# Moving one split of a down operand ahead, and dealing out the last norm of group 2 chunk by chunk

## The chip, the cores and the metric

The kernel runs on one core of a Trainium2 chip. The metric is the device time of one execution in microseconds (us); the time given is the median of three executions. A further execution was taken by the hardware profiler, and every duration below comes from that one.

## The reference, cut to what matters

One layer of a decoder trunk, for 1024 prompt tokens and 32 decode tokens, 1056 in all, with a model width of 1024. Behind the mixing sub-layer come a SwiGLU feed-forward part (2816 hidden channels) and a per-layer input:

```
x = x + rms(mix, n_mix_post)
f = rms(x, n_ffn_pre)
f = (silu(f @ w_gate) * (f @ w_up)) @ w_down
x = x + rms(f, n_ffn_post)
x = x + sigmoid(x @ w_ple_gate) * (p @ w_ple)
```

`rms(x, g)` is x times 1 / sqrt(mean of x squared + 1e-6), times a gain for each channel.

## The kernel before

**Tiling.** Everything is kept with the channels on the 128 partitions and the tokens along the free dimension. The 1056 tokens are three groups of 352. Each fp32 operand is split into a high part of the type fp32r and the rest (`split`, L172 to L174: ScalarE makes the high part at L173, VectorE the low part at L174). A product is three matmuls: high by high, high by low, low by high. All matmuls are issued at L128, in the order in which the code is written (`pinned`). A product of 352 columns fills one of eight PSUM banks, and a bank is free again when VectorE or ScalarE has taken its result.

**Groups 0 and 1** go through Strassen's scheme in Winograd's form: `seven` computes a 2 by 2 block product with seven products in place of eight, from the operands B11, B21, B22 and four differences T1 to T4. The weights need sums too (`w_sums`): four additions on GpSimd (L1108), then a split into `sh` and `sl`. **Group 2** goes the direct way.

**Feed-forward.** The hidden channels come in five slabs of four blocks of 128, and a rest of two. A step `pair` makes one block for groups 0 and 1: gate and up products are the two block rows of one `seven`, and their product goes into `hidf` (`hf`, L1215, for the rest blocks L1217). When the four pairs of a slab are done, its seven down operands (`hp`) are made from `hidf`: B11, B21 and B22 are splits, T1 to T4 a subtraction in place (L1183) and a split. The steps `dn_pair` multiply them with the down weights and add the results into `accp` (`ap`, L1278, on VectorE; in slab 0 a copy on ScalarE, L1280). The down pairs of slab s-1 stand behind pairs 1 and 2 of slab s; those of the last slab stand behind the two pairs of the rest.

**What sets the order.** Long jobs of VectorE and ScalarE that are not part of a step run as chains (`chain`). Each is a Python generator. After each product `turn(n)` adds n matmuls to a clock and lets every chain go on whose time has come. A chain yields `load, wait`: it goes on when VectorE, taken to have a certain share of its time for chains (`share`, 0.9 in the pairs, 0.5 in the last part), has worked off `load` matmuls' worth of work and `wait` more matmuls have passed. What the generator issues is so written between the products. A scheduler then orders the instructions of each engine other than TensorE, and can hoist one that is ready, except where the order is held (`fix`). `h_operands` is such a chain, started behind a slab's fourth pair.

**The last part.** `ple_pair` multiplies groups 0 and 1 with `w_ple_gate` through `seven`; each result gets a sigmoid, a product with the embedding (`embed`, L1401) and the residual (L1403), and is stored. Beside it runs the chain `one_steps` for group 2: `x2_steps` sums squares (`rstd_steps`: short matmuls into one bank, a root, a reciprocal), spreads the root over the partitions with two matmuls against ones (`dg`), multiplies the feed-forward output by it (L1354, 1408 wide, twice), and adds it to the residual with the gain in eight chunks of 352 (L1357), then makes the split operand (`fh`, `fl`) of each half. The steps `ple_one` for group 2 follow.

Of the kernel before, what the change touches and what calls it, by code (L numbers as in the profile page):

```python
# [36 lines left out]
SLAB = 4  # L37
NSLAB = FFC // SLAB
# [24 lines left out]
def trunk_kernel(  # L63
# [44 lines left out]
    def nm(s):  # L108
        cnt[0] += 1
        return f"{s}{cnt[0]}"  # L110

    def act_tile(shape, dt=F32, s="a"):
        return apool.tile(shape, dt, tag="a", bufs=A_SLOTS, name=nm(s))
# [12 lines left out]
    def mm(*args, **kw):  # L126

        ins = te.matmul(*args, **kw)  # L128
        if pinned[0]:
            tc.keep_in_program_order(ins)  # L130

    def bank():
        return psum.tile([P, 512], F32, tag="b", name=nm("b"))
# [181 lines left out]
    def need(k, ahead=LOOK):  # L315

        for i in range(len(made), min(k + ahead + 1, len(ITEMS))):
            kind, js = ITEMS[i]
            if kind == "direct":
                w_split(js[0])  # L320
                made[i] = pairs[js[0]]
            elif kind == "half":
                w_load(js[0])
                hl = two_in_one([P, 4, P])
                split(*hl, raws[js[0]][:, 4:8, :])
                made[i] = hl
            elif kind == "small":
                w_load(js[0])
                hl = two_in_one([P, 2, 256])
                split(*hl, raws[js[0]])  # L330
                made[i] = hl
            else:
                made[i] = w_sums(*(raws[ITEMS[j][1][0]] for j in js))
            for kind, js in ITEMS[i + 1 : i + 3]:
                if kind != "sums":
                    w_load(js[0])
        return made[k]
# [48 lines left out]
    def rstd_steps(acc, wait=14):  # L386
        w = acc.shape[1] // 4
        sm = bank()
        for j in range(4):
            mm(sm[32 * j : 32 * j + 32, :w], ones[:, :32], acc[:, j * w : (j + 1) * w], start=True, stop=True)  # L390
        t = act_tile([P, 2 * (TB * P + w)], F32R, "dg")
        dgs = [t[:, h * TB * P : h * TB * P + 4 * w] for h in range(2)]
        hl = t[:, 2 * TB * P :].rearrange("p (h k) -> p h k", h=2)
        sd = spool.tile([P, w], F32, tag="sw", name=nm("sw"))
        se.activation(sd, sm[:, :w], AF.Sqrt, bias=epst, scale=1.0 / D)
        ve.reciprocal(sd, sd)
        ve.tensor_copy(hl[:, 0], sd)
        ve.tensor_tensor(hl[:, 1], sd, hl[:, 0].bitcast(F32), op=ALU.subtract)
        lead = ident[:, ::32].unsqueeze(2).to_broadcast([P, 4, w])
        for h in range(2):  # L400
            part = hl[:, h].bitcast(F32).unsqueeze(1).to_broadcast([P, 4, w])
            ve.tensor_tensor(dgs[h].rearrange("p (i k) -> p i k", i=4), lead, part, op=ALU.mult)
        yield 6, wait
        ps = bank()
        for h in range(2):
            mm(ps[:, : 4 * w], ones_r, dgs[h], start=h == 0, stop=h == 1)
        return ps[:, : 4 * w]
# [598 lines left out]
    def chain(steps, wait=0, alone=False):  # L1006

        chains.append([steps, now[0] + wait, alone])
# [128 lines left out]
    def seven(items, x7, done):  # L1137

        ig, iu, is_ = items[:3]
        wg = need(ig)  # L1140
        p1 = tmp(N, "p1")
        se.copy(p1, product(quarter(wg, 0), x7["B11"]))
        c11 = tmp(N, "c11")
        add(c11, p1, product(quarter(wg, 1), x7["B21"]))
        done("C11", c11)
        p4 = product(need(iu), x7["T4"])
        s = need(is_)
        add(p1, p1, product(s["S2"], x7["T2"]))
        u3 = tmp(N, "u3")
        add(u3, p1, product(s["S3"], x7["T3"]))  # L1150
        c21 = tmp(N, "c21")
        add(c21, u3, p4)
        done("C21", c21)
        p5 = product(s["S1"], x7["T1"])
        add(u3, u3, p5)
        add(p1, p1, p5)
        done("C22", u3)
        add(p1, p1, product(s["S4"], x7["B22"]))
        done("C12", p1)
# [3 lines left out]
    hidf = {}  # L1163
# [13 lines left out]
    def h_operand(name, src):  # L1177
        t = act_tile([P, 2, 2, N], F32R, "hp")
        split(t[:, 0], t[:, 1], src)
        h7[name] = t[:, 0], t[:, 1]  # L1180

    def h_sum(name, out, a, b):
        ve.tensor_tensor(out, a, b, op=ALU.subtract)  # L1183
        h_operand(name, out)

    def h_operands():
        b11, b21, b12, b22 = (hidf[g][:, 2 * k : 2 * k + 2, :] for g in (0, 1) for k in range(2))
        for name, b in (("B11", b11), ("B21", b21), ("B22", b22)):
            h_operand(name, b)
            yield 6, 0  # L1190
        for name, *args in (
            ("T1", b11, b12, b11),
            ("T3", b12, b22, b12),
            ("T2", b22, b22, b11),
            ("T4", b21, b21, b22),
        ):
            h_sum(name, *args)
            yield 11, 0

    def do_pair(s, i, items):  # L1200

        t = {}

        def done(which, c):
            t[which] = c
            if which in ("C11", "C12"):
                se.activation(c, c, AF.Silu)
            if which == "C21" and i == 0:
                finish(list(chains))
                for g in (0, 1) if s < NSLAB else ():  # L1210
                    hidf[g] = half(g, s="hf")
            for g, a, b in ((0, "C21", "C11"), (1, "C22", "C12")):
                if which == ("C21", "C12")[g]:
                    if s < NSLAB:
                        ve.tensor_tensor(hidf[g][:, i, :], t[a], t[b], op=ALU.mult)  # L1215
                    else:
                        ve.tensor_tensor(t[a], t[a], t[b], op=ALU.mult)  # L1217
                        hid_put(g, s, i, t[a])

        seven(items, f7, done)  # L1220
        if s < NSLAB and i == SLAB - 1:
            chain(h_operands(), 6)

    def do_one(s, i, items):
        if (s, i) == (AHEAD, 0):
# [100 lines left out]
    acc3 = []  # L1326
# [19 lines left out]
    def x2_steps(g, operand):  # L1346

        for h in range(2):
            x2[g][h] = half(g, s="x2")
            nc.sync.dma_start(x2[g][h], x1d[g][h])  # L1350
        r = yield from rstd_steps(acc3[g], 22)
        for h in range(2):
            yh, xh = os_[g][h], x2[g][h]
            ve.tensor_tensor(yh, yh, bc4(r), op=ALU.mult)  # L1354
            for c in range(4):
                k = 4 * h + c
                ve.scalar_tensor_tensor(  # L1357
                    xh[:, c, :], yh[:, c, :], gn[:, 3, k : k + 1], xh[:, c, :], op0=ALU.mult, op1=ALU.add
                )
                if c % 2:  # L1360
                    yield 12, 0
            operand(g, h, xh)
            yield 10, 0
# [173 lines left out]
```

## Time and profile before

| what | us |
|---|---|
| median of three executions | 1079.05 (1078.88 to 1079.31) |
| the profiled execution | 1080.58 |
| its span | 1078.79 |
| VectorE busy in it | 874.7 |
| ScalarE busy | 510.2 |
| GpSimd busy | 281.3 |

The span runs from the first to the last instruction that the profiler recorded; the execution's own time has 1.79 us around it. Rows of the timeline give the start, the duration, the engine (PE is TensorE, DVE VectorE, ACT ScalarE, POOL GpSimd), the line, the operation, what it writes and reads by the program's names, the shapes, the number of merged instructions, and in brackets the idle time ahead of it and what ended that. Matmuls overlap, so a distance between starts says more of TensorE than a duration.

### The profile page before, as it was taken

The numbers are of one execution on the slowest core, as the hardware profiler recorded it, in microseconds if no ns is written. First come the engines' busy times: TensorE is split into PE (matmuls) and PEld (weight loads), VectorE is DVE, ScalarE is ACT, GpSimd is POOL, SyncE is SP. The second block draws the span as 40 slices with busy tenths as digits, with TensorE's granted clock in tenths as the row PEclk, the third lists the DMA queues.
The fourth block names the chain that finished last, engine by engine and source line by source line (L and its number), as shares of the span: only waits on it lengthen the run. The fifth ranks groups of instructions, "written<-read, shape, count | busy, mean of one in ns | idle before, by whom it ended". The sixth has DMA issues, their size and how long they took to land. (4 is left out here: it accounts for less than half of the span.)

```text
span 1078.8 us, 18189 instructions
## 1 busy us (share of the span) xinstructions
PE 1069.6 (99%) x7107; PEld 1053.0 (98%) x7107; DVE 874.7 (81%) x1303; ACT 510.2 (47%) x872; POOL 281.3 (26%) x211
## 2 busy tenths in 40 slices
PE   8999999999999999999999999999999999999998
PEld 8999988899999999999999999999999999999998
DVE  6876378886979957796598898898899998969983
ACT  7423277664555533445543343344344455545431
POOL 0063032200000023454454454444442000023200
PEclk9999999999999999999999999999999999999999
DMA  8121311544543432412212212213235556464361
GB/s 299 57 74 39 102 58 37 201 159 144 201 168 131 137 98 78 152 60 93 84 60 98 79 59 98 80 59 106 73 112 182 186 160 244 152 214 162 98 201 60
DMA packets 43575, 130.91 MB, mean 121 GB/s; under 512 B 5061, under 2 KB 15717, under 8 KB 43489
## 3 DMA queue, kind: packets, MB, share of 16 engines
q1 hardware_dynamic: 42160, 127.98, 35.0%
q10 hardware_dynamic: 1328, 1.77, 0.5%
q8 instruction: 56, 0.92, 0.4%
q14 instruction: 31, 0.25, 0.1%
HBM read 113.86 MB, written 15.87 MB: 120 GB/s over the span
## 5 line engine op out<-in xcount | busy, mean ns | idle before, releaser
L1108 POOL TENSOR_TENSOR wr<-wr,wr 128x512 f32<-128x512 f32 x108 | 174.9, 1634 | 476.8 <-DMA wr<-in_w_gu_dram 238.1
L173 ACT CAST wh<-wr 128x1024 fp32r<-128x1024 f32 (+1 forms) x138 | 142.1, 1031 | 162.8 <-PE b L128 98.7
L174 DVE TENSOR_TENSOR wl<-wr,wh 128x1024 fp32r<-128x1024 f32 (+1 forms) x138 | 171.0, 1241 | 42.0 <-ACT wh L173 26.3
L128 PE MATMUL b<-fh,wh 128*128 128x352 f32 x624 | 201.7, 323 | 0.8 <-DVE p L1135 0.8
L128 PE MATMUL b<-fh,wl 128*128 128x352 f32 x624 | 200.1, 321 | 0.0
L128 PE MATMUL b<-fl,wh 128*128 128x352 f32 x624 | 200.0, 320 | 0.0
L173 ACT CAST sh<-wr 128x1024 fp32r<-128x1024 f32 x72 | 75.7, 1052 | 141.3 <-POOL wr L1108 138.9
L128 PE MATMUL b<-fh,sh 128*128 128x352 f32 x416 | 134.3, 323 | 0.0
L128 PE MATMUL b<-fl,sh 128*128 128x352 f32 x416 | 133.2, 320 | 0.0
L128 PE MATMUL b<-fh,sl 128*128 128x352 f32 x416 | 133.2, 320 | 0.0
L174 DVE TENSOR_TENSOR sl<-wr,sh 128x1024 fp32r<-128x1024 f32 x72 | 97.4, 1353 | 37.4 <-ACT sh L173 24.5
L128 PEld LDWEIGHTS b<-fh,wh 128*128 128x128 f32 x624 | 117.0, 187 | 1.5 <-DVE p L1135 1.1
L128 PEld LDWEIGHTS b<-fl,wh 128*128 128x128 f32 x624 | 117.5, 188 | 0.0
L128 PEld LDWEIGHTS b<-fh,wl 128*128 128x128 f32 x624 | 116.9, 187 | 0.0
L128 PE MATMUL b<-h,wh 128*128 128x352 f32 x480 | 105.9, 326 | 1.2 <-ACT h L449 1.1
L128 PE MATMUL b<-hid,wh 128*128 128x352 f32 x416 | 99.6, 322 | 0.0
L128 PEld LDWEIGHTS b<-h,wh 128*128 128x128 f32 x480 | 82.4, 190 | 2.5 <-ACT h L449 1.2
L1108 POOL TENSOR_TENSOR wr<-wr 128x512 f32<-128x512 f32 x36 | 50.9, 1414 | 106.7 <-DVE w L174 106.7
L128 PEld LDWEIGHTS b<-fl,sh 128*128 128x128 f32 x416 | 78.2, 188 | 0.0
L128 PEld LDWEIGHTS b<-fh,sh 128*128 128x128 f32 x416 | 78.0, 187 | 0.1
L128 PEld LDWEIGHTS b<-fh,sl 128*128 128x128 f32 x416 | 77.9, 187 | 0.0
L128 PE MATMUL b<-hp,sh 128*128 128x352 f32 x320 | 76.6, 322 | 0.9 <-DVE ap L1278 0.9
(202 smaller groups left out, 2220.7 us busy)
## 6 DMA issues: line engine op xcount, KB each, us to landing
wr<-in_w_gu_dram SPq DMA_DIRECT2D x88, 512.0 KB, 3.3
wr<-in_w_dn_dram SPq DMA_DIRECT2D x40, 512.0 KB, 3.3
wr<-in_w_pg_dram SPq DMA_DIRECT2D x16, 512.0 KB, 3.6
x<-in_x_dram SPq DMA_DIRECT2D x6, 704.0 KB, 8.6
x1d<-x SPq DMA_DIRECT2D x6, 704.0 KB, 3.6
x<-x1d SPq DMA_DIRECT2D x6, 704.0 KB, 5.1
out_y_dram<-yo SPq DMA_DIRECT2D x24, 176.0 KB, 2.3
wr<-in_w_out_b_dram SPq DMA_DIRECT2D x8, 512.0 KB, 3.3
```

The source lines that it names most:

```text
L128: ins = te.matmul(*args, **kw)
L173: fix(se.copy(hi, src))
L174: fix(ve.tensor_tensor(lo, src, hi.bitcast(F32), op=ALU.subtract))
L1108: ge.tensor_tensor(out, a, b, op=op)
```

## The change

Three edits. The chain `h_operands` is cut in two: `h_first` (B11 and T1) starts ahead of the products of a slab's fourth pair, `h_rest` (the other five) behind them as before. The wait between the sums and the spread of group 2's last norm goes from 22 to 14 matmuls (with the load of 6, at a share of 0.5, the spread comes 30 matmuls' worth after the sums, in place of 38). And in that norm each chunk yields for itself, with a load of 6, where two chunks yielded together with a load of 12. No instruction is added or taken away.

```
-    def h_operands():
-        b11, b21, b12, b22 = (hidf[g][:, 2 * k : 2 * k + 2, :] for g in (0, 1) for k in range(2))
-        for name, b in (("B11", b11), ("B21", b21), ("B22", b22)):
+    def h_parts():
+        return (hidf[g][:, 2 * k : 2 * k + 2, :] for g in (0, 1) for k in range(2))
+
+    def h_first():
+        b11, _, b12, _ = h_parts()
+        h_operand("B11", b11)
+        yield 6, 0
+        h_sum("T1", b11, b12, b11)
+        yield 11, 0
+
+    def h_rest():
+        b11, b21, b12, b22 = h_parts()
+        for name, b in (("B21", b21), ("B22", b22)):
             h_operand(name, b)
             yield 6, 0
         for name, *args in (
-            ("T1", b11, b12, b11),
             ("T3", b12, b22, b12),
             ("T2", b22, b22, b11),
             ("T4", b21, b21, b22),
...
+        if s < NSLAB and i == SLAB - 1:
+            chain(h_first(), 6)
         seven(items, f7, done)
         if s < NSLAB and i == SLAB - 1:
-            chain(h_operands(), 6)
+            chain(h_rest(), 6)
...
-        r = yield from rstd_steps(acc3[g], 22)
+        r = yield from rstd_steps(acc3[g], 14 if g == 2 else 22)
...
-                if c % 2:
+                if g == 2:
+                    yield 6, 0
+                elif c % 2:
                     yield 12, 0
```

The order of the instructions on VectorE shows at three places what moves. The first is the end of the second down pair of slab 3, ahead of the fourth pair of slab 4, in the kernel before (`hf_7532` is the half of `hidf` that T1 is made of; the split that makes B11 of it stands a few rows above the first one):

```order
L1183 TENSOR_TENSOR hf_7532<-hf_7533,hf_7532 128x704
L1278 TENSOR_TENSOR ap_5329<-ap_5329,b_8048 128x352
L174 TENSOR_TENSOR sl_8001<-wr_7879,sh_8000 128x1024
L1278 TENSOR_TENSOR ap_5329<-ap_5329,b_8056 128x352
L1278 TENSOR_TENSOR ap_5346<-ap_5346,b_8064 128x352
L1278 TENSOR_TENSOR ap_5346<-ap_5346,b_8072 128x352
L1278 TENSOR_TENSOR ap_5363<-ap_5363,b_8080 128x352
L174 TENSOR_TENSOR sl_8007<-wr_7834,sh_8006 128x1024
```

and in the changed kernel (L1289 is the eviction that was L1278):

```order
L1183 TENSOR_TENSOR hf_7532<-hf_7533,hf_7532 128x704
L1289 TENSOR_TENSOR ap_5329<-ap_5329,b_8048 128x352
L174 TENSOR_TENSOR sl_8001<-wr_7879,sh_8000 128x1024
L1289 TENSOR_TENSOR ap_5329<-ap_5329,b_8056 128x352
L1289 TENSOR_TENSOR ap_5346<-ap_5346,b_8064 128x352
L1289 TENSOR_TENSOR ap_5346<-ap_5346,b_8072 128x352
L174 TENSOR_TENSOR hp_8134<-hf_7532,hp_8134 128x704
L1289 TENSOR_TENSOR ap_5363<-ap_5363,b_8080 128x352
L174 TENSOR_TENSOR sl_8007<-wr_7834,sh_8006 128x1024
```

T1's subtraction stands in the same row in both; its split, `hp_8134`, is new here. The other slabs look the same.

The second is the first pair behind the last slab, where the other operands are made, before (`hp_8295`, `hp_8316` and `hp_8338` are B22, T1 and T3; the L1183 rows make T2 and T4; `w` is the half split of a second weight, `c_8335` the eviction of the T4 product):

```order
L174 TENSOR_TENSOR wl_8160<-wr_8099,wh_8159 128x1024
L1135 TENSOR_TENSOR c_8249<-p_8231,b_8250 128x352
L174 TENSOR_TENSOR w_8226<-wr_8144,w_8226 128x512
L174 TENSOR_TENSOR hp_8295<-hf_7533,hp_8295 128x704
L174 TENSOR_TENSOR hp_8316<-hf_7532,hp_8316 128x704
L1135 TENSOR_TENSOR p_8231<-p_8231,b_8302 128x352
L174 TENSOR_TENSOR hp_8338<-hf_7533,hp_8338 128x704
L1183 TENSOR_TENSOR hf_7533<-hf_7533,hf_7532 128x704
L174 TENSOR_TENSOR sl_8271<-wr_8144,sh_8270 128x1024
L1135 TENSOR_TENSOR u_8320<-p_8231,b_8321 128x352
L1183 TENSOR_TENSOR hf_7532<-hf_7532,hf_7533 128x704
L1135 TENSOR_TENSOR c_8335<-u_8320,b_8282 128x352
```

and in the changed kernel (B22, T3, T2 and T4 are `hp_8270`, `hp_8303`, `hp_8339` and `hp_8346`):

```order
L174 TENSOR_TENSOR wl_8167<-wr_8099,wh_8166 128x1024
L174 TENSOR_TENSOR w_8233<-wr_8151,w_8233 128x512
L174 TENSOR_TENSOR hp_8270<-hf_7533,hp_8270 128x704
L1135 TENSOR_TENSOR c_8256<-p_8238,b_8257 128x352
L174 TENSOR_TENSOR hp_8303<-hf_7533,hp_8303 128x704
L1135 TENSOR_TENSOR p_8238<-p_8238,b_8310 128x352
L1183 TENSOR_TENSOR hf_7533<-hf_7533,hf_7532 128x704
L1183 TENSOR_TENSOR hf_7532<-hf_7532,hf_7533 128x704
L174 TENSOR_TENSOR sl_8278<-wr_8151,sh_8277 128x1024
L174 TENSOR_TENSOR hp_8339<-hf_7533,hp_8339 128x704
L1135 TENSOR_TENSOR u_8324<-p_8238,b_8325 128x352
L174 TENSOR_TENSOR hp_8346<-hf_7532,hp_8346 128x704
```

T1's split is gone from here, the half split w stands one row earlier, and the eviction of the T4 product (now `c_8343`) comes two rows below the last one shown. In the pair behind this one, the half split w and the product of the gates (L1217, now L1226) have changed places.

The third is the last part, ahead of the eviction (`p_10548`, `p_10547` in the changed kernel) that takes the S2 product of the third `ple_pair`; before:

```order
L174 TENSOR_TENSOR fl_10578<-x_10403,fh_10577 128x1408
L1403 TENSOR_TENSOR yo_10535<-p_10340,xm_10055 128x352
L174 TENSOR_TENSOR w_10583<-wr_10432,w_10583 128x512
L1135 TENSOR_TENSOR c_10563<-p_10548,b_10564 128x352
L1354 TENSOR_TENSOR o_8808<-o_8808,b_10490 128x1408
L1401 TENSOR_TENSOR c_10563<-c_10563,b_10586 128x352
L174 TENSOR_TENSOR w_10597<-wr_10546,w_10597 128x512
L1403 TENSOR_TENSOR yo_10594<-c_10563,xm_10538 128x352
L1357 SCALAR_TENSOR_TENSOR x_10405<-o_8808,c_72,x_10405 128x352 x2
L1135 TENSOR_TENSOR p_10548<-p_10548,b_10629 128x352
```

and in the changed kernel (L1354, L1357, L1401 and L1403 are L1365, L1368, L1414 and L1416):

```order
L1365 TENSOR_TENSOR o_8808<-o_8808,b_10473 128x1408
L1414 TENSOR_TENSOR p_10340<-p_10340,b_10526 128x352
L174 TENSOR_TENSOR wl_10542<-wr_10388,wh_10541 128x1024
L1416 TENSOR_TENSOR yo_10534<-p_10340,xm_10055 128x352
L174 TENSOR_TENSOR fl_10578<-x_10403,fh_10577 128x1408
L1135 TENSOR_TENSOR c_10563<-p_10547,b_10564 128x352
L174 TENSOR_TENSOR w_10583<-wr_10432,w_10583 128x512
L1414 TENSOR_TENSOR c_10563<-c_10563,b_10586 128x352
L1368 SCALAR_TENSOR_TENSOR x_10405<-o_8808,c_72,x_10405 128x352
L1416 TENSOR_TENSOR yo_10594<-c_10563,xm_10537 128x352
L174 TENSOR_TENSOR w_10597<-wr_10545,w_10597 128x512
L1135 TENSOR_TENSOR p_10547<-p_10547,b_10629 128x352
```

The second multiply by the spread root now stands ahead of six rows that it stood behind, one of the two chunks that stood right ahead of the eviction stands behind it, and the half split `w_10597` is now the row just ahead of it. Further up, the first multiply (`o_8807`) and the first two chunks stand ahead of the eviction of the T1 product, where they stood behind it. On TensorE only the two spreading matmuls move, eight matmuls ahead.

## The prediction

> **What bounds the kernel now.** I read the page's head first, then the busy time by stretches, then what TensorE waited for behind 340 us, then the instructions one by one at each of those waits.
>
> ```profile
> span 1078.8 us, 18189 instructions
> PE 1069.6 (99%) x7107; PEld 1053.0 (98%) x7107; DVE 874.7 (81%) x1303; ACT 510.2 (47%) x872; POOL 281.3 (26%) x211
> ```
>
> TensorE is idle for 1078.8 - 1069.6 = 9.2 us of the whole span, so nothing but those 9.2 us can be won without taking matmuls out, and the change takes none out. The stretches say where they lie (the second number is TensorE's busy time in the stretch):
>
> ```profile
> 0.00:50.00 50.00, 47.16 (x282) 45.60 (x283) 36.01 (x66) 30.43 (x52) 2.54 (x19) 0.97 0.54 183
> ...
> 800.00:850.00 50.00, 49.10 (x306) 48.46 (x305) 48.68 (x68) 20.76 (x26) 11.31 (x7) 1.00 0.41 149
> 1000.00:1050.00 50.00, 49.17 (x307) 48.88 (x306) 45.17 (x67) 20.27 (x30) 7.02 (x4) 1.00 0.49 153
> 1050.00:1079.00 29.00, 24.68 (x154) 24.40 (x152) 10.28 (x16) 5.57 (x10) 0.00 (x0) 1.00 0.20 68
> ```
>
> 2.84 us go at the start, and 4.1 in the last stretch, whose window reaches 0.2 past the span's end; 0.9 lie near 800 and 0.83 near 1000, and the 0.5 that are left over lie elsewhere. The edits touch only the stretches near 800 and 1000. The waits of TensorE behind 340 us (us in total, times, longest) are just these two places:
>
> ```profile
> PE b L128 <- DVE ap L1278: 0.9, 2, 0.6
> PE b L128 <- DVE p L1135: 0.8, 1, 0.8
> ```
>
> Matmuls overlap, so the true loss is read from the starts:
>
> ```profile
> 815.16 0.48 PE L128 MATMUL b<-hp,sh 128*128 128x352 f32 x2
> 815.48 0.32 PE L128 MATMUL b<-hp,sl 128*128 128x352 f32 x1
> 816.40 0.59 PE L128 MATMUL b<-hp,sh 128*128 128x352 f32 x2 [0.60 <-DVE ap L1278]
> ...
> 830.65 0.32 PE L128 MATMUL b<-hp,sl 128*128 128x352 f32 x1
> 831.28 0.59 PE L128 MATMUL b<-hp,sh 128*128 128x352 f32 x2 [0.30 <-DVE ap L1278]
> ...
> 1016.41 1.12 PE L128 MATMUL b<-pl,w 128*128 128x352 f32 x6
> 1018.36 0.43 PE L128 MATMUL b<-fh,wh 128*128 128x352 f32 x1 [0.83 <-DVE p L1135]
> 1018.62 0.32 PE L128 MATMUL b<-fl,wh 128*128 128x352 f32 x1
> ```
>
> Two matmuls from 815.16 to 815.48: 0.16 each. So the first stall is 816.40 - 815.64 = 0.76, the second 831.28 - 830.81 = 0.47, the third 1018.36 - (1016.41 + 6 x 0.16) = 1.0. Behind each, one more start comes 0.1 late (1018.62 - 1018.36 = 0.26 in place of 0.16). Together **2.5 us**: all that this change can win. Each is a wait for a PSUM bank (there are 8): the product that starts at 816.40 needs the bank of the product eight before it, and VectorE is late in evicting that one. So VectorE's order and pace decide at both places, and nowhere else.
>
> **First edit: B11 and T1 beside the fourth pair.** Read against the rows of the order, it does less than it says. In the order of before, B11's low part and T1's subtraction stand already beside the second down pair, ahead of the fourth pair: the scheduler had hoisted them. Only T1's own split moves, one VectorE and one ScalarE instruction per slab, five in all; none is added.
>
> ```profile
> L174 DVE TENSOR_TENSOR hp<-hf,hp x35: 876/885/1989, 423.6 to 796.8; 128x704 fp32r<-128x704 f32 x35
> ...
> 785.49 2.79 DVE L174 TENSOR_TENSOR hp<-hf,hp 128x704 fp32r<-128x704 f32 x2
> 790.12 1.98 DVE L1183 TENSOR_TENSOR hf<-hf,hf 128x704 f32<-128x704 f32 x1
> 792.02 1.21 DVE L174 TENSOR_TENSOR sl<-wr,sh 128x1024 fp32r<-128x1024 f32 x1
> 794.82 0.88 DVE L174 TENSOR_TENSOR hp<-hf,hp 128x704 fp32r<-128x704 f32 x1
> 797.56 1.60 DVE L1217 TENSOR_TENSOR c<-c,c 128x352 f32<-128x352 f32 x1
> 801.96 0.68 DVE L174 TENSOR_TENSOR w<-wr,w 128x512 fp32r<-128x512 f32 x1
> 805.39 1.50 DVE L174 TENSOR_TENSOR sl<-wr,sh 128x1024 fp32r<-128x1024 f32 x1 [0.31 <-ACT sh L173]
> 815.84 2.66 DVE L1278 TENSOR_TENSOR ap<-ap,b 128x352 f32<-128x352 f32 x6
> 822.07 1.23 DVE L174 TENSOR_TENSOR sl<-wr,sh 128x1024 fp32r<-128x1024 f32 x1 [0.55 <-ACT sh L173]
> 830.71 1.37 DVE L1278 TENSOR_TENSOR ap<-ap,b 128x352 f32<-128x352 f32 x3
> ```
>
> An instruction on VectorE begins 0.08 before its forerunner ends (790.12 + 1.98 against 792.02), so a split of 704 costs 0.80, of 1024 1.13, of 512 0.60, an eviction 0.43 (2.66 for six). In slabs 0 to 3 TensorE waits for none of this, so there the edit is worth nothing, and ScalarE, 47% busy, pays its 0.7 from idle time. In the last slab VectorE is behind from 782 on. I go through its new order from 782.51, where the old one stands at b12 - b22: 0.81, wl 1.13, w 0.60, B22 0.80, eviction 0.43, T3 caught by GpSimd as the second one at 785.49 was (1.91), eviction 0.43, two subtractions caught (1.5 and 1.9 as at 790.12), sl 1.13, T2 0.80, eviction 0.43, T4 0.80, sl 1.13, eviction 0.43. The product of the gates then starts at 796.75 in place of 797.56: **0.8 earlier**, the one split that left.
>
> Half of it is lost at once. In the pair behind, the half split w now stands one row later, behind the product with the second gate (0.45). GpSimd's weight sums start when w ends,
>
> ```profile
> 802.78 1.50 POOL L1108 TENSOR_TENSOR wr<-wr 128x512 f32<-128x512 f32 x1 [3.99 <-DVE w L174]
> ```
>
> ScalarE casts their result, and VectorE's sl at 805.39 already waits for that cast. So w ends 0.4 earlier, not 0.8, and sl, with everything queued behind it (the pair's last evictions and those of the down products), comes 0.4 earlier. The second chain of the kind (w, sums, cast, sl at 822.07 with 0.55 of waiting) moves with it. TensorE's last bank there is freed by the evictions at 830.71, so place one is worth **-0.4**: the first stall shrinks from 0.76 to about 0.4, the second stays. Bounds: -1.3 if VectorE is 1.3 earlier there, which takes the whole 0.8 and a caught instruction less (0.7 to 1.1 each); +0.7 if one more is caught.
>
> **Second and third edit: group 2's norm.** The two spreading matmuls come 8 matmuls (1.3 us) sooner, so the multiply by them (L1354, 1.61) moves ahead of T4's eviction, and the eight chunks of the norm (L1357) are dealt out singly.
>
> ```profile
> 994.75 0.51 DVE L1135 TENSOR_TENSOR u<-p,b 128x352 f32<-128x352 f32 x1
> ...
> 1005.06 1.07 DVE L1357 SCALAR_TENSOR_TENSOR x<-o,c,x 128x352 f32<-128x352 f32 x2
> ...
> 1009.16 1.61 DVE L1403 TENSOR_TENSOR yo<-p,xm 128x352 f32<-128x352 f32 x1
> ...
> 1011.73 1.61 DVE L1354 TENSOR_TENSOR o<-o,b 128x1408 f32<-128x1408 f32 x1
> ...
> 1014.73 3.15 DVE L1357 SCALAR_TENSOR_TENSOR x<-o,c,x 128x352 f32<-128x352 f32 x2
> 1017.80 0.51 DVE L1135 TENSOR_TENSOR p<-p,b 128x352 f32<-128x352 f32 x1
> ```
>
> ```profile
> 996.35 2.56 POOL L1108 TENSOR_TENSOR wr<-wr,wr 128x512 f32<-128x512 f32 x2
> 1007.79 2.59 POOL L1108 TENSOR_TENSOR wr<-wr,wr 128x512 f32<-128x512 f32 x1 [8.89 <-DVE p L1401]
> 1014.51 1.44 POOL L1108 TENSOR_TENSOR wr<-wr 128x512 f32<-128x512 f32 x1 [4.12 <-DVE w L174]
> 1016.03 2.98 POOL L1108 TENSOR_TENSOR wr<-wr,wr 128x512 f32<-128x512 f32 x2
> ```
>
> The third stall ends with the eviction at 1017.80. Ahead of it stood six chunks, the last two of them during GpSimd's sums: 3.15 where two cost 1.07 alone, 1.04 extra each. In the new order the same work stands ahead of it less one chunk, and the w that starts those sums is now the row just before it, so the fifth chunk comes while GpSimd is idle. From 994.75: eviction 0.45, multiply 1.53, eviction 0.43, two chunks that meet the sums of 996.35 and end about 0.35 behind them (999.25), two evictions 0.86, chunk 0.5, two splits 2.26, four short ones 1.7, eviction 0.43, chunk 0.5, multiply 1.53, 0.43, wl 1.13, yo caught as at 1009.16 (1.53), fl 1.53, 0.43, w 0.60, 0.43, chunk 0.5, 0.43, w 0.60: the eviction starts near 1014.8 and ends at 1015.3. TensorE needs the bank at 1017.36. So the stall goes, with 2 us to spare: **-1.1**. What is late next: three chunks now meet GpSimd's sums behind it, each in front of one eviction; by the same steps T1's eviction (the p half) ends near 1023.6, and its bank is wanted at 1024.05 by a TensorE that is no longer held. That 0.45 is the thinnest cover. SyncE's queue moves too: the load of p and one weight load come ahead of an output; no TensorE wait hangs on either.
>
> **Sum.** -1.1 - 0.4 = -1.5. The profiled execution took 1080.58 (its span 1078.79 and 1.79 around it) and would take 1079.1; the median shown is 1.53 below it, so **1077.6**. With the bounds of the first edit 1076.7 to 1078.7.
>
> **Rivals.** (a) *All three stalls go.* If VectorE keeps the 0.8 and sheds a caught instruction, the second stall goes as well: 1079.05 - 1.1 - 1.3 = 1076.7. Against it: the sl that waits for the cast. 11%.
>
> (b) *The third stall stays, because single chunks catch GpSimd more often.* Three caught chunks more, 1.04 each, eat the 2 us of cover, and 0.4 of T1's cover goes with one: 1078.7. For it: two chunks do meet the sums near 997. Against it: GpSimd has nothing between 999 and 1007.8, and its next trio waits for a w that now stands behind the fifth chunk. 13%. The Trainium skill, page "SBUF — State Buffer", section "SBUF: two separate sides", speaks for this rival: the port pair that VectorE and GpSimd share is an exclusive lock for a whole instruction, and whoever comes second is fully blocked, so a chunk put singly in front of an eviction can hold that eviction for a whole GpSimd instruction. The trace agrees on the blocking (1.04 extra per caught chunk); with a fair split of the port I would expect the two at 997 to end 0.2 or so sooner, which changes no stall.
>
> (c) *Slower: the weight sums fall behind.* The later w stands behind the gate product in all five slabs, not the last alone. In slab 3 the first of these evictions ends 0.4 before the product that wants its bank:
>
> ```profile
> 734.58 1.80 DVE L1278 TENSOR_TENSOR ap<-ap,b 128x352 f32<-128x352 f32 x4
> ...
> 735.49 0.48 PE L128 MATMUL b<-hp,sh 128*128 128x352 f32 x2
> ```
>
> (734.58 + 0.51 = 735.09.) If the chain from w over GpSimd and ScalarE to sl ends more than 0.4 later than now, TensorE waits there too. With one GpSimd instruction held up for its whole 1.5 and VectorE's own lead lost, sl comes about 1.6 later: 1.2 in each of slabs 1 to 3, if all are as tight as this one, 1.6 in the last, 5.2 in all, less 1.1: 1083.2. It decides from a sl later than 805.8. Against it: VectorE is 0.8 ahead when it gets there. 7%.
>
> (d) *The change does nothing measurable to either place*: a part of (b) and of the forecast's lower bound, since B11 and T1 had moved already.
>
> **How the numbers follow.** Forecast 69%, (a) 11%, (b) 13%, (c) 7%. About 0.2% (2.2 us) is what a measurement of this kernel can tell from no change; the forecast and (b) lie within it, (a) just beyond. Faster 0.11, same 0.82, slower 0.07. The range runs from (a) to a little above (b) and no change: 1076.6 to 1079.3; it leaves out (c) and the far edge of (a).
>
> **What would show it.** Right: no wait of TensorE near 1017; T1's split (hp) beside the second down pair; sl near 805.0, still waiting for sh; the wait at 815.6 about half; that near 830 still there. Wrong: a new TensorE wait between 1019 and 1026 (b), waits for ap in slabs 1 to 3 (c), or no wait at all behind 340 us (a).

## The result, and the profile after

| | kernel before | changed kernel |
|---|---|---|
| median (range) of 12 executions each, us | 1079.18 (1078.35 to 1081.66) | 1076.91 (1075.84 to 1078.35) |
| ratio, with its 95% interval | | 0.9979 (0.9971 to 0.9987) |
| the profiled execution, us | 1080.58 | 1077.23 |
| its span, us | 1078.79 | 1075.4 |

The changed kernel is 2.27 us faster, where 1.5 was forecast. The time lies within the range given, just beyond the 0.2% that can be told from no change, and nearest to rival (a), in which all three stalls go.

The head of the changed kernel's page:

```profile
span 1075.4 us, 18180 instructions
PE 1068.5 (99%) x7107; PEld 1051.6 (98%) x7107; DVE 872.4 (81%) x1303; ACT 512.2 (48%) x872; POOL 275.6 (26%) x211
```

Its busy time by stretches (the length of the stretch, then the busy time of TensorE, its weight loads, VectorE, ScalarE and GpSimd, each with the number of instructions, then the granted clock):

```profile
800.00:850.00 50.00, 50.00 (x315) 49.74 (x314) 47.79 (x67) 20.01 (x24) 11.12 (x7) 1.00 0.39 135
1000.00:1050.00 50.00, 50.00 (x315) 50.00 (x314) 44.23 (x66) 20.80 (x30) 8.26 (x4) 1.00 0.51 161
```

Behind 340 us TensorE no longer waits for anything by the view of its waits, which lists nothing: both stretches are full, where 0.90 and 0.83 were idle. The starts show more, since overlapping matmuls hide a short wait. Place one in the changed kernel, first VectorE and then TensorE:

```profile
795.60 1.63 DVE L1226 TENSOR_TENSOR c<-c,c 128x352 f32<-128x352 f32 x1
...
800.45 0.68 DVE L174 TENSOR_TENSOR w<-wr,w 128x512 fp32r<-128x512 f32 x1
...
803.88 1.34 DVE L174 TENSOR_TENSOR sl<-wr,sh 128x1024 fp32r<-128x1024 f32 x1 [1.21 <-ACT sh L173]
...
814.03 2.66 DVE L1289 TENSOR_TENSOR ap<-ap,b 128x352 f32<-128x352 f32 x6
```

```profile
829.18 0.32 PE L128 MATMUL b<-hp,sl 128*128 128x352 f32 x1
829.48 0.59 PE L128 MATMUL b<-hp,sh 128*128 128x352 f32 x2
```

From 324 to 811 us the two traces run alike but for a shift: TensorE of the changed kernel is 0.53 ahead, which came about in the first 250 us, where the change does nothing. To compare, take 0.53 off the times of before. The gate product c then starts 1.43 earlier (797.03 against 795.60), sl 0.98, the six evictions 1.28. The first stall is gone, the second is 0.14 (829.48 - 829.18 = 0.30 where 0.16 is the rule).

Not all of that lead comes from the rows that the edit moves. The last eviction into `hidf`, ahead of them, starts 0.29 earlier already (781.41 in that time against 781.12); before and after:

```profile
781.94 0.54 DVE L1215 TENSOR_TENSOR hf<-u,p 128x352 f32<-128x352 f32 x1 [0.56 <-ACT p L1207]
```

```profile
781.12 0.55 DVE L1224 TENSOR_TENSOR hf<-u,p 128x352 f32<-128x352 f32 x1 [0.56 <-ACT p L1216]
```

Place two, VectorE again. TensorE stands 2.29 ahead of the trace of before when it reaches this part (984.23 against 986.52 for the same matmul):

```profile
1012.47 0.50 DVE L1135 TENSOR_TENSOR p<-p,b 128x352 f32<-128x352 f32 x1
1012.89 1.46 DVE L1368 SCALAR_TENSOR_TENSOR x<-o,c,x 128x352 f32<-128x352 f32 x1
...
1020.97 0.51 DVE L1135 TENSOR_TENSOR p<-p,b 128x352 f32<-128x352 f32 x1
```

The S2 eviction ends at 1012.97, in the time of before 1015.26; 1015.3 was forecast. The stall behind it is gone. T1's p half ends at 1023.77 in that time, where 1023.6 was forecast. But there is a new, short wait, which the prediction did not have. It is that of the two spreading matmuls for dg. GpSimd, VectorE and TensorE:

```profile
989.66 1.29 POOL L1108 TENSOR_TENSOR wr<-wr,wr 128x512 f32<-128x512 f32 x1 [9.85 <-DMA wr<-in_w_pg_dram]
...
990.38 0.64 DVE L397 CAST dg<-sw 128x88 fp32r<-128x88 f32 x1
991.05 0.25 DVE L398 TENSOR_TENSOR dg<-sw,dg 128x88 fp32r<-128x88 f32 x1
991.21 0.95 DVE L402 TENSOR_TENSOR dg<-c,dg 128x352 fp32r<-128x352 f32 x2
...
991.88 0.77 PE L128 MATMUL b<-dg,c 128*128 128x352 f32 x2
```

Two matmuls in 0.77 where 0.48 is the rule: 0.29 lost, since dg came late.

So far it looks as if the third stall had given 0.8 and the first two 1.2. That is the reading of one trace of each kernel, and the experiments show how far it carries.

### The profile page after: what moved, and what is told of

Read it like the earlier page. It is cut to its first block, busy times and chain, and to the rows that moved or that the text cites. A ratio compares the mean times of both kernels' runs of the same rounds, so it can differ in the third digit from the quotient of the medians.

```text
span 1075.4 us, 18180 instructions
## 1 busy us (share of the span) xinstructions
PE 1068.5 (99%) x7107; PEld 1051.6 (98%) x7107; DVE 872.4 (81%) x1303; ACT 512.2 (48%) x872; POOL 275.6 (26%) x211
## 4 chain that ended last, share of the span: by engine, by line
PE 95%; ACT 2%; DVE 2%; DMA 0%; issue 0%; SPq 0%; ACTq 0%; DVEq 0%
PE b L128 95%; ACT a L732 1%; DMA xr<-in_x_dram 0%; DVE mx L721 0%; PE b L122 0%; DVE a L779 0%; DVE wl L174 0%; DVE ml L712 0%; ACT wh L173 0%; DVE sm L737 0%; DVE a L781 0%; ACT y L914 0%; ACT sq L902 0%; ACT y L922 0%; ACT es L729 0%
## 5 line engine op out<-in xcount | busy, mean ns | idle before, releaser
L1108 POOL TENSOR_TENSOR wr<-wr,wr 128x512 f32<-128x512 f32 x108 | 170.0, 1588 | 480.0 <-DMA wr<-in_w_gu_dram 247.9
```

The lines of the kernel that those rows point to most:

```text
L1108: ge.tensor_tensor(out, a, b, op=op)
```

## The experiments

The runs came in three sets, each on another chip. Within a set each kernel was timed in five rounds against the kernel before on the same chip, and profiled once. All texts on what was expected stood before the runs.

### The edits apart

Only the first edit (h_first and h_rest kept, the norm as before):

```
-        r = yield from rstd_steps(acc3[g], 14 if g == 2 else 22)
+        r = yield from rstd_steps(acc3[g], 22)
...
-                if g == 2:
-                    yield 6, 0
-                elif c % 2:
+                if c % 2:
                     yield 12, 0
```

> The kernel before with the first edit alone (B11 and T1 beside the fourth pair; the norm's wait stays 22 and its chunks go in pairs). Theory A (VectorE gains about 1 us in the last slab, its late evictions there come earlier): TensorE's stalls near 815 and 830 shrink from 1.3 us together to about 0.15, the stall of 1.1 us near 1017 stays as it was. The matmuls behind the stall near 830 also go back from one per 0.1611 us to one per 0.1589, worth 0.5 more up to the next gap at 866. Together 1.2 to 1.7 less than the kernel before. Rival B (the first edit is worth the 0.4 of the forecast, and the rest of the difference between the two traces is the start-up and chance): a stall of about 0.4 near 815 and one of 0.5 near 830 are left, and the time is 0.4 less.

The second and third edit without the first (the kernel before, with the two hunks above the other way round):

> The kernel before with the second and third edit alone (wait 14, single chunks). Theory A: the two stalls near 815 and 830 stay at 1.3 us together; the stall near 1017 goes, and a wait of about 0.3 us for dg appears at the second spreading matmul: 0.8 less in gaps, and 0.3 to 0.8 less by the pace of the matmuls to the end, so 0.8 to 1.6 less than the kernel before. Rival C (the edits need each other, since VectorE comes to the last part late without the first one): the eviction of the S2 product still ends behind the need of its bank, a stall of 0.5 or more is left near 1017, and the time is at most 0.4 less.

The second alone, and the third alone:

> The kernel before with the second edit alone (wait 14; chunks in pairs). The eviction of the S2 product then stands behind one chunk more than in the changed kernel, and that chunk meets GpSimd's sums (1.46 where 0.57 is a chunk alone). Theory A: that eviction had 4.5 us to spare in the changed kernel, so 1.4 later does no harm: no stall near 1017, the wait for dg near 992 is there, the time is that of the second and third edit together within 0.2. Rival D (the single chunks are what removes the stall): a stall of 0.3 or more is left near 1017.

> The kernel before with the third edit alone (wait 22; single chunks). In the order the multiply by the root stands where it stood, but no chunk stands ahead of the eviction of the S2 product any more, where two did that took 3.15 us. Theory A: that eviction ends near 1015.2, 2 us ahead of the need: no stall near 1017, and no wait for dg either, since the spreading matmuls stand where they stood: 1.1 less in gaps, and with the quick pace (one matmul per 0.1589 us) kept to the end 0.7 more: 1.1 to 1.9 less than the kernel before, so better than the second and third edit together by 0.3 or more. Rival E (the earlier multiply is what removes the stall): a stall of 0.3 or more is left near 1017.

| kernel | median, us | kernel before, us | ratio (95%) |
|---|---|---|---|
| first edit | 1077.45 | 1078.69 | 0.9988 (0.9979 to 0.9996) |
| second and third | 1078.68 | 1078.69 | 0.9998 (0.9990 to 1.0007) |
| second | 1078.30 | 1078.69 | 0.9995 (0.9986 to 1.0003) |
| third | 1078.29 | 1078.69 | 0.9997 (0.9988 to 1.0005) |

The first edit gives 1.24, three times its forecast. The others alone give nothing that can be told. Theory A is right on the first edit and too high on the others, and C and D fall with it: neither with the second and third edit together nor with the second alone did TensorE wait near 1017. (The 4.5 us to spare in the text on the second edit is too much: in the changed kernel that eviction ends at 1012.97 and the matmul that needs its bank starts at 1015.53, 2.6 later. Nor was the wait for dg, which that text expected, in the trace of the second alone.) Rival E falls in part: with the third alone the eviction of the S2 product is in time, but a wait turns up 30 matmuls later. TensorE in that kernel, where L1403 is the product with the embedding (L1401 in the kernel before):

```profile
1021.74 0.40 PE L128 MATMUL b<-fh,w 128*128 128x352 f32 x1 [0.20 <-DVE c L1403]
```

That is rival (b) of the prediction: three single chunks that meet GpSimd's sums (1.18 each in place of 0.57) stand between the evictions behind 1014, two splits sl follow, and c at L1403, behind all of them, is late. In the changed kernel c stands ahead of the two splits.

### The same kernels again, and one edit taken back

The changed kernel and the kernel before were run again, with the changed kernel less its third edit, and less its second:

```
-                if g == 2:
-                    yield 6, 0
-                elif c % 2:
+                if c % 2:
                     yield 12, 0
```

```
-        r = yield from rstd_steps(acc3[g], 14 if g == 2 else 22)
+        r = yield from rstd_steps(acc3[g], 22)
```

> The changed kernel once more, beside the others of this set. Theory A (the edits act at separate places and add up): its gain is that of the first edit alone (1.2) and of the second and third together (0 to 0.8), 1.2 to 2.1 less than the kernel before. Theory F (which instructions GpSimd holds up differs from execution to execution, so one trace is one draw): the sizes of the waits in its trace differ from the first trace's by some 0.3 us at one place or more: a wait for dg of 0 to 0.6, not of 0.28 again, and a stall near 829 of 0 to 0.5.

> The changed kernel with its chunks dealt out in pairs again (first and second edit). Theory A: the second edit alone removes the stall near 1017, as it did without the first; the wait for dg is there if GpSimd's sum holds up the cast of dg (L397, 0.20 alone), up to 0.6, and not otherwise. Time that of the changed kernel within 0.5. Rival D (the single chunks are needed once VectorE is early): a stall of 0.3 or more between 1010 and 1026, and 0.5 or more above the changed kernel.

> The changed kernel with the wait of 22 again (first and third edit). Theory A: no wait for dg, since the spreading matmuls stand 12 matmuls later, with 1.85 us between dg and them as in the kernel before; three chunks that meet GpSimd's sums stand between the evictions behind 1014, as in the run with the third edit alone, so a wait of up to 0.5 near 1019 to 1022 remains; 0.5 less to 0.5 more than the changed kernel. Rival E (the wait of 14 is what helps): a stall of 0.8 or more there, and 0.5 or more above the changed kernel.

> The kernel before against itself. Its time is the same within 0.3, which is what such a comparison can tell. Theory F (which instructions GpSimd holds up differs from execution to execution): its stalls near 815, 830 and 1017 stand at the same three places but differ from those of the first trace (0.76, 0.47 and 1.0) by some 0.3 us at one place or more; if all three come out the same within 0.05, the theory falls. The matmuls behind each stall go one per 0.1589, 0.1600 or 0.1611 us, with nothing between, until the next gap.

| kernel | median, us | kernel before, us | ratio (95%) |
|---|---|---|---|
| changed kernel, again | 1076.92 | 1079.18 | 0.9977 (0.9966 to 0.9987) |
| first and second edit | 1076.82 | 1079.18 | 0.9975 (0.9966 to 0.9985) |
| first and third edit | 1076.66 | 1079.18 | 0.9977 (0.9969 to 0.9986) |
| kernel before, against itself | 1079.15 | 1079.18 | 1.0001 (0.9990 to 1.0011) |

The gain holds, and either of the two later edits may be left out without a difference that can be told; no version clearly beats the changed kernel. D and E fall in their time. With the first and third the wait behind the chunks is there again, at 1019.4 and 0.47 in all, within what A gave it. The traces bear out theory F, most of all that of the kernel before, whose second profiled execution took 1077.12 us, against 1080.58 the first time. TensorE's waits in it behind 340 us:

```profile
engine line waited for: us in total, times, longest us
PE b L128 <- DVE ap L1278: 0.3, 1, 0.3
```

The stall near 1017, which the prediction priced at 1.1, isn't there. Why, its VectorE and GpSimd show:

```profile
1005.82 1.62 DVE L174 TENSOR_TENSOR fl<-x,fh 128x1408 fp32r<-128x1408 f32 x1
1007.36 0.52 DVE L1403 TENSOR_TENSOR yo<-p,xm 128x352 f32<-128x352 f32 x1
1007.79 0.68 DVE L174 TENSOR_TENSOR w<-wr,w 128x512 fp32r<-128x512 f32 x1
...
1014.91 0.51 DVE L1135 TENSOR_TENSOR p<-p,b 128x352 f32<-128x352 f32 x1
```

```profile
1005.95 3.68 POOL L1108 TENSOR_TENSOR wr<-wr,wr 128x512 f32<-128x512 f32 x1 [8.85 <-DVE p L1401]
```

In the first trace of before fl started here:

```profile
1007.62 1.62 DVE L174 TENSOR_TENSOR fl<-x,fh 128x1408 fp32r<-128x1408 f32 x1
```

GpSimd's sum came 0.17 behind that (1007.79), waited for the end of fl, went ahead of yo, and yo took 1.61 in place of 0.52. In the second it came 0.13 behind the start of fl, and VectorE's yo and w went ahead of it: the sum took 3.68 where 1.29 is one alone, and yo 0.52. VectorE is 1.09 earlier for it, and the S2 eviction is in time. In the trace of the first edit alone the sum came ahead of fl and fl took 2.48; the stall was 0.61 there:

```profile
1004.74 2.48 DVE L174 TENSOR_TENSOR fl<-x,fh 128x1408 fp32r<-128x1408 f32 x1
```

So the size of the stall hangs on a race that the order of the program doesn't settle. (A second one is told behind the table of all traces.)

### What is left: where the first edit acts, the sum of the edits, and the wait for dg

Four last runs. The first edit in the last slab alone (shown against the code of the changed kernel; the norm is as before):

```
-        if s < NSLAB and i == SLAB - 1:
+        if s == NSLAB - 1 and i == SLAB - 1:
             chain(h_first(), 6)
         seven(items, f7, done)
         if s < NSLAB and i == SLAB - 1:
-            chain(h_rest(), 6)
+            chain(h_rest(s < NSLAB - 1), 6)
...
-    def h_rest():
+    def h_rest(both):
...
-        for name, b in (("B21", b21), ("B22", b22)):
+        for name, b in ([("B11", b11)] if both else []) + [("B21", b21), ("B22", b22)]:
...
-        for name, *args in (
+        for name, *args in ([("T1", b11, b12, b11)] if both else []) + [
```

> The kernel before with the first edit in the last slab alone (in slabs 0 to 3 all seven operands are made behind the fourth pair, as before). Theory A (TensorE waits for VectorE only behind the last slab): the time is that of the first edit in all five slabs, 1.0 to 1.6 less than the kernel before; no gap of TensorE between 324 and 800 us in either; stalls of at most 0.3 together near 815 and 829. Rival H (slabs 0 to 3 give part of it): 0.6 or less.

The second and third edit alone, and the first alone, once more:

> Second and third edit alone, a second time, since the sum of the edits alone (1.24 and 0.0) fell short of the three together (2.3). Theory A (separate places, the rest chance): with both sets together the second and third edit come out at 0.5 to 1.0 less than the kernel before, and with the first edit's 1.2 to 1.5 they reach the 2.3 within 0.4. Rival I (the edits need each other): again 0.3 or less.

> First edit alone, a second time. Theory A: 1.2 to 1.5 less than the kernel before again; its trace shows the stall near 1015 or not, as the two traces of the kernel before did (1.1 and none), since what decides it, whether GpSimd's sum or VectorE's next row goes first behind the split fl, is not set by the code. Rival I (the edits need each other): a gain of 1.0 or less, and the stall near 1015 there again.

And the changed kernel with the cast of dg on another engine:

```
-        ve.tensor_copy(hl[:, 0], sd)
+        se.copy(hl[:, 0], sd)
```

> The changed kernel with the cast of dg (L397) on ScalarE in place of VectorE, in all norms. Theory J (the wait for dg near 992 comes from GpSimd's sum holding up that cast on VectorE: 0.64 and 0.90 where it was there, 0.20 in the run without a wait): the cast takes about 0.2 to 0.3 on ScalarE whatever GpSimd does, dg is ready at least 0.3 ahead of where it was, and there is no wait of TensorE near 992, unless one of the next three rows of VectorE is held up in its place. Rival K (the spread simply stands too early for the chain of root, reciprocal, cast and two multiplies): a wait of 0.1 or more stays. The time is that of the changed kernel less at most 0.5, within what can be told.

| kernel | median, us | kernel before, us | ratio (95%) |
|---|---|---|---|
| first edit, last slab alone | 1077.40 | 1078.69 | 0.9990 (0.9981 to 0.9998) |
| second and third, again | 1078.28 | 1078.69 | 0.9996 (0.9987 to 1.0005) |
| cast of dg on ScalarE | 1076.96 | 1078.69 | 0.9989 (0.9980 to 0.9998) |
| first edit, again | 1077.61 | 1078.69 | 0.9992 (0.9983 to 1.0001) |

**Where it acts.** In the last slab alone the edit gives 1.29, as in all five (1.24 and 1.08). H falls, as the prediction had it: no trace has a gap of TensorE between 324 and 800 us.

**The sum.** Over all executions the medians are 1078.90 for the kernel before (120 of them), 1077.51 with the first edit (33, with the run of the last slab alone), 1078.38 with the other two (23), 1076.92 with all three (20): 1.39 + 0.52 = 1.91 against 1.98. (One execution of the kernel before, of 6041.9 us, is left out.) That would say that the edits add up, but it mixes sets: the kernel before stood at 1079.18 where the three edits together were timed, and at 1078.69 where the others were. Each against the kernel before of its own set, the first edit gave 1.24, 1.08 and 1.29, the other two 0.01 and 0.41, and all three 2.27 and 2.26, some 0.8 more than the sum. In the last set alone, with the cast moved, all three gave 1.73, where 1.08 or 1.29 and 0.41 make 1.49 or 1.70. The two runs that asked it gave 0.41 and 1.08, each between what A and what I expected. So whether the edits add up is not shown.

**The wait for dg.** On ScalarE the cast took 0.27 while GpSimd's sum ran until 990.77:

```profile
989.47 1.30 POOL L1108 TENSOR_TENSOR wr<-wr,wr 128x512 f32<-128x512 f32 x1 [9.44 <-DVE w L174]
```

```profile
990.60 0.27 ACT L397 CAST dg<-sw 128x88 fp32r<-128x88 f32 x1 [1.26 <-DVE sw L396]
```

```profile
990.90 0.25 DVE L398 TENSOR_TENSOR dg<-sw,dg 128x88 fp32r<-128x88 f32 x1 [0.33 <-ACT dg L397]
991.06 0.95 DVE L402 TENSOR_TENSOR dg<-c,dg 128x352 fp32r<-128x352 f32 x2
```

There was no wait of TensorE for dg. Counted from the same matmul (984.44 here, 984.23 there), dg was ready 0.36 earlier than in the changed kernel's first trace (L402 ended at 992.01 and 992.16), as J had it. That is only 0.08 ahead of the spread, which started at 992.09: VectorE stood idle 0.33 until the cast was handed back. The time can't be told from the changed kernel's. What tells J from K is the set of traces with the cast on VectorE. The changed kernel's second trace has no wait:

```profile
990.92 0.20 DVE L397 CAST dg<-sw 128x88 fp32r<-128x88 f32 x1
```

GpSimd's sum, 1.41 long from 989.28, was over there before the cast began. In the six traces with the early spread and the cast on VectorE the cast took 0.20, 0.20, 0.44, 0.58, 0.64 and 0.90, and TensorE lost 0, 0, 0.10, 0.24, 0.29 and 0.57. The wait grows with the cast, from about 0.35 on. So J explains the wait, and K is half right: without a collision the spread fits with some 0.1 to spare.

### All traces side by side

What TensorE lost at each place is worked out from the starts of its 7107 matmuls, which every trace has. Place one is the time from the 5265th to the 5771st (80.40 in the changed kernel's second trace, 860.80 - 780.40, which has no gap there), place two from the 6561st to the last (85.98, 1070.75 - 984.77). The losses are above these two, and how much of each is gaps stands in brackets:

```
                             place one     place two
without the first edit
  before                     1.95 (1.48)   1.87 (1.10)   norm as before
  before, again              0.90 (0.89)   0.00          norm as before
  second and third           0.98 (0.78)   1.12 (0.57)
  second and third, again    1.24 (0.82)   0.11 (0.10)
  second                     2.04 (1.56)   0.00
  third                      0.83 (0.83)   0.43 (0.44)
with the first edit
  first                      0.10 (0.10)   1.49 (0.72)   norm as before
  first, again               0.00          0.31 (0.31)   norm as before
  first, last slab alone     0.00          0.00          norm as before
  all three                  0.25 (0.24)   0.84 (0.29)
  all three, again           0.00          0.00
  all three, cast on ACT     0.00          0.00
  first and second           0.00          0.78 (0.24)
  first and third            0.00          0.48 (0.47)
```

**The second race at place two.** In the five traces with the norm as before, two things account for when the S2 eviction starts: how long the cast of dg takes, which GpSimd's sum near 990 holds up in some executions, and what the sum near 1006 does to fl and yo. Start of the S2 eviction from the 6561st matmul on, and, above the last row, the length of the cast and of fl and yo together:

```
                          eviction   cast     fl, yo   both    gaps
before                    31.28      +0.20    +1.09    1.29    1.10
first                     30.89      +0.06    +0.86    0.92    0.72
first, again              30.48      +0.49     0.00    0.49    0.31
before, again             29.99       0.00     0.00    0.00    0.00
first, last slab alone    29.98       0.00     0.00    0.00    0.00
```

The cast in the first trace of before and in the second of the first edit:

```profile
992.67 0.40 DVE L397 CAST dg<-sw 128x88 fp32r<-128x88 f32 x1
```

```profile
990.48 0.69 DVE L397 CAST dg<-sw 128x88 fp32r<-128x88 f32 x1
```

So the stall that was 1.1 in the trace on which the forecast rests is the sum of two draws, and goes where neither is bad.

**In the mean.** Place one: 1.32 in the mean of the six without the first edit, 0.04 of the eight with it. Place two: 0.73 in the mean of the five with the norm as before, 0.41 of the five with both later edits (the cast moved in one). The first edit takes away a loss that is always there; the others mostly trade one loss that is there at times for another.

## Why the prediction was right in its range, and wrong in its parts

**The places** were right: VectorE's late evictions near 815, 830 and 1017, and nowhere else.

**The first edit was mis-sized: -0.4 forecast, about -1.3 measured.** What failed is the lead of VectorE, and with it that of w and sl. The loss on the way from the gate product to w was as forecast: 0.45 of the lead of c goes there (from the start of c to the end of w 5.08 before and 5.53 now). But c led by 1.43 in the two first traces, where 0.8 was forecast, and sl by 0.98, where 0.4 was. The step that failed is T3, "caught by GpSimd as the second one at 785.49 was (1.91)". It took 1.55, so 1.47 less the overlap, 0.44 under its term:

```profile
785.48 1.55 DVE L174 TENSOR_TENSOR hp<-hf,hp 128x704 fp32r<-128x704 f32 x1
```

All traces say the same. From the start of hf to the start of w VectorE takes 20.0 us in each of the six traces without the edit and 19.15 to 19.34 in the eight with it, 0.65 to 0.85 less where 0.4 was forecast. The rows held up by GpSimd on that way cost 4.0 above their length alone in each of the six, four rows of 0.7 to 1.1 (the gate product is one of them, or a fourth split in its place), and 3.3 to 3.4 in the eight. So 0.5 to 0.7 of waiting was shed beside the split that left. Why GpSimd holds up the new order less stays open.

The rest is a draw that the prediction took for a fixture: how late VectorE already is at hf. Counted from the start of place one, hf starts at 1.80 and 2.02 in the two traces without the edit that lost most in gaps (1.48 and 1.56), and at 1.24 to 1.44 in the four that lost 0.78 to 0.89; with the edit it starts at 1.24 to 1.50. The 0.29 of the two first traces is of this kind, and no run shows that the edit brings it. The prediction had -1.3 as a bound and as rival (a), at 11%. In time that is the case that came.

**The second and third edit: the mechanism was right, the price was not.** The S2 eviction and T1's p half came within 0.2 of the forecast, and three chunks met GpSimd's sums as said. That it came so near is in part luck: yo, taken as caught (1.53), was not (0.52), and the half split w, taken at 0.60, was (1.35). (The recorded steps add up to 1014.64 for the start of the eviction, not to 1014.8; measured, in the time of before, it is 1014.76.) Two steps failed. First, -1.1 took the third stall for a fixture, and it was one draw: of five traces with that order two have it large (1.10 and 0.72 in gaps), one has 0.31, two have none. Second, "the two spreading matmuls come 8 matmuls (1.3 us) sooner" was read from the difference of the waits, 22 and 14, as was the sentence on TensorE ahead of the prediction. Work goes in only between products, so they stand 12 matmuls sooner, ahead of a whole product, which is 12 x 0.159 = 1.9 us. In the trace of before dg is ready at 994.22 and the spread starts at 996.07: 1.85 of cover, all of it used up:

```profile
993.27 0.95 DVE L402 TENSOR_TENSOR dg<-c,dg 128x352 fp32r<-128x352 f32 x2
```

```profile
996.07 0.48 PE L128 MATMUL b<-dg,c 128*128 128x352 f32 x2
```

The prediction named the multiply behind the spread and the queues, but not the chain ahead of it.

**The sum** of -1.5 was as near the -2.27 as it is by luck: the errors have opposite signs, the first edit too small by some 0.9, the other two (0.0 to 0.5 by the medians) too large. The step from the profiled execution to the median (1.53 lower) hid the same error: that execution lay above the median since its stalls were large, so they could not be taken off the median whole.

**The rivals.** (a) came in its time, 1076.7 against 1076.91, and at place one half in its mechanism: most of a caught instruction was shed (0.5 to 0.7), but the 0.8 was not kept whole, since c to w took 0.45 more. (b) does not come in the changed kernel, but does with the third edit without the second. (c) didn't come: no slab ahead of the last shows a gap. Of the signs given, T1's split stands where it was said (hp at 765.08, 0.88), and sl waits for sh as before, but at 804.41 in the time of before, where 805.0 was said; the wait near 815 went whole, where half was said.

## What to carry to other kernels

Price a stall from several executions: a wait that ends on a row which another engine can hold up is a draw, and taking it off the median whole counts it twice; two traces of one kernel tell it. Where VectorE and GpSimd share work on SBUF, an order that takes a row away from a stretch in which GpSimd runs can be worth that row and part of a collision more. And read how far a step moves from the order on every engine that it issues to, then look for what must be ready ahead of it.

## What the runs showed of the hardware that was not expected

**Who goes first.** A sum of GpSimd that waits behind a row of VectorE goes next in some executions (yo 1.61, the sum 2.59 with its wait), and in others after two more rows of VectorE (yo 0.52, the sum 3.68). The Trainium skill, page "SBUF — State Buffer", section "SBUF: two separate sides", has the one that starts first hold the shared ports for its whole instruction; the traces agree: behind a sum that started 0.31 ahead of it, fl took 2.48 where 1.62 is one alone. Which of two that wait comes next that section leaves open, and at this place that decides about 1 us.

**What was not held up.** Behind 400 us the 5210 rows of VectorE of 128x352 that read a PSUM bank and an SBUF tile took 0.50 to 0.53 in all 14 traces, whatever GpSimd did. Rows of that size with both inputs in SBUF took up to 1.67 in place of 0.52.

**A stall can cost more than its gap.** Behind 324 us the matmuls of 352 columns follow each other in one of three paces and nothing between: one per 0.1589, 0.1600 or 0.1611 us, as means over 80 to 3400 starts. A pace changes only at a gap of TensorE, and holds until the next. Behind the third stall of the first trace of before it was 0.1611 to the end: 346 x 0.00222 = 0.77 beside the gaps of 1.10. Behind the wait for dg in the changed kernel's first trace it was 0.1600 to the end: 491 x 0.0011 = 0.54 beside 0.29. The counts of the stretches show it, 832 to 864 and 1020 to 1070, with the granted clock at 1.00 throughout; the first trace of before:

```profile
832.00:864.00 32.00, 32.00 (x201) 32.00 (x200) 31.97 (x48) 13.71 (x23) 0.00 (x0) 1.00 0.57 204
...
1020.00:1070.00 50.00, 50.00 (x312) 50.00 (x311) 33.39 (x54) 19.08 (x29) 0.00 (x0) 1.00 0.45 145
```

and the changed kernel's second trace, which has no stall:

```profile
832.00:864.00 32.00, 32.00 (x204) 32.00 (x203) 31.97 (x49) 14.43 (x25) 0.00 (x0) 1.00 0.53 188
...
1020.00:1070.00 50.00, 50.00 (x317) 50.00 (x316) 31.47 (x49) 16.26 (x26) 0.00 (x0) 1.00 0.43 148
```

TensorE counts as fully busy in both, with three and five matmuls fewer. Which pace follows a gap is not its length: 0.63 was followed by 0.1611 in the first trace of before, 0.64 by 0.1589 in the second. Behind the short sums of the norms it was 0.1589 wherever it was read behind 324 us, in all 14 traces. What sets it was not tried and stays open.
